# A projection's quads of v and z taken apart: v alone and z alone, with the context's v by seven products in two heads of four

## The chip, the cores and the metric

The kernel runs on one core of a Trainium2 chip. The metric is the device time of one execution in microseconds, the median of several runs. All matrix products run as float32r matmuls on TensorE; VectorE (DVE) and ScalarE (ACT) prepare their operands and drain their results; GpSimd (POOL) issues the stores of intermediate results, SyncE (SP) the loads.

## The reference

Two layers over 512 latent tokens (x) and 256 context tokens (ctx) of width 1024. Layer 0 is a bidirectional multi-scale retention with four heads, layer 1 a chunked gated MLP on the latent tokens. What matters here is the projection at the start of layer 0:

```python
def retention_project(h, w_in):
    a, bq, cq = RET_QK_WIDTH, 2 * RET_QK_WIDTH, 2 * RET_QK_WIDTH + RET_WIDTH
    q = to_heads(h @ w_in[:, :a], RET_HEADS)
    k = to_heads(h @ w_in[:, a:bq], RET_HEADS) * (RET_QK_DIM ** -0.5)
    v = to_heads(h @ w_in[:, bq:cq], RET_HEADS)
    z = h @ w_in[:, cq:]
    return q, k, v, z
```

For each head q and k have 256 columns, v and z have 512. The latent tokens need q, k, v and z. The context tokens need only k and v: layer 1 is the last one and reads no context, so the context's q, z and output are not computed.

## The kernel before

**Quads.** The projection is cut into twelve quads. A quad is a weight block of 1024 rows by 512 columns, cut in quarters B11, B12, B21, B22 of 512 x 256 (first digit: the half of the rows, second digit: the half of the columns). A quad of kind `kq` has k's columns of one head in one half and q's in the other. A quad of kind `vz` has 256 of v's columns in one half and 256 of z's in the other, so each head has two `vz` quads. `QUADS` fixes the order.

**Seven products.** The latent tokens' side is cut in quarters A11 to A22 of 256 tokens by 512 rows of the contraction. Instead of eight products of quarters a quad does seven (a Strassen-Winograd scheme): B11, B21, B22 as they are and four differences T1 to T4 of quarters, each with an operand of the tokens' side: A11, A12, A22 or one of the sums S1 to S4 (`WITH`). Class `Product` runs them in the order `SINGLE` and keeps the running sums: a `snap` is a ScalarE copy of a PSUM bank, `plus` a VectorE addition of a bank to an earlier snap; a result quarter is passed to `done`. The first quad, `kq` of head 0, is done plainly with eight products.

**The context beside it.** For `kq` and `vz` quads the context's k or v is needed for the first half of columns only. `beside` does it plainly: the context's 256 tokens (`hc`) with B11, and with B21, each a product of 24 matmuls, added in one bank.

**Halves.** Every operand of a matmul is split into a high half (ScalarE, a cast to float32r) and a low half (VectorE, what the cast left out), and every pair of 128-row operands takes three matmuls (`mm3`): low x high, high x low, high x high. So one product of quarters is 4 x 2 x 3 = 24 matmuls of 128 x 256. The weights' halves stand in one of four `hl` tiles; `Stream.upto` makes them two products ahead of their use, `Stream.sum` makes the differences T1 to T4 in place in the loaded quarters (`raw`, VectorE, 128 x 1024).

**Order of the work.** TensorE's order is that of the text. VectorE's and ScalarE's instructions of this stage are ordered by the scheduler, except for work put in with `aside`, which stays behind what stands before it in the text. After the first quad come two quads run in turns (`pair`, order `PAIRED`); there the sums S2, S3, S4 and the decay logarithms are made as well. Then a loop runs the other nine quads one by one, n = 0 to 8, and does side work between the products: `popped` (the rotary embedding, "rope", of a `kq` quad's results, mostly in the quad behind it), `step` (background: a piece of the modulation vectors, five steps in a quad), `decay(0)` at n = 5 (tables of the decays: exponentials on ScalarE, products on VectorE), `load_qk(0)` from n = 6 and `load_v(0)` at n = 8 (operands of the first head's attention).

**Stores.** `v_d`, `vc_d`, `z_d` are places in device memory, per head; `spill` stores to them through POOL's queue. z goes through SiLU on ScalarE first. Places in on-chip memory are laid out once, in the order of the calls of `lay`; a tile is named by its tag there.

Of the kernel before, what the change touches and what calls it, by code (L numbers as in the profile page):

```python
# [8 lines left out]
F32R = mybir.dt.float32r  # L9
# [4 lines left out]
P = 128  # L14
# [53 lines left out]
def hybrid_kernel(ctx, tc, xT_d, cT_d, cv_d, sv_d, rows_d, ada0_d, adag_d, w_d, rope_d, dec_d, ws_d, id_d, out_d):  # L68
# [21 lines left out]
    def lay(sizes, bufs=1):  # L90
        for tag, n in sizes.items():
# [3 lines left out]
         "sq0": 16, "sq1": 16, "sq2": 16, "rs0": 1024, "rs1": 1024, "rs2": 1024, "shb": 16, "gate0": 32, "gs1": 32,  # L95
# [59 lines left out]
    class Stream:  # L155
# [40 lines left out]
        def upto(self, n, late=None):  # L196

            while self.done < min(n, self.limit or len(self.items)):
                q, name, uses, at, place = self.items[self.done]
                self.pump()  # L200
                r = self.raws[q, at]
                self.sum(self.done)
                hl = place() if place else hl_tile(q[0] in ("vz", "v1"))
# [65 lines left out]
    QUADS = (("kq", 0), ("vz", 0, 0), ("vz", 0, 1), ("vz", 1, 0), ("vz", 1, 1), ("kq", 1), ("vz", 2, 0), ("vz", 2, 1),  # L269
             ("kq", 2), ("vz", 3, 0), ("kq", 3), ("vz", 3, 1))  # L270
# [73 lines left out]

    class Product:
# [3 lines left out]
        def __init__(self, product, done, side=None):  # L349
            self.product, self.done, self.side, self.s = product, done, side, {}  # L350

        def snap(self, key, bank):
            t = self.s[key] = t2("snap")
            act.copy(t, bank)
# [6 lines left out]
        def beside(self, name, w):  # L361
            if self.side is None:
                return
            if name == "B11":
                self.c = pt()
                self.product(self.c, self.side[:, :, 0:4, :], w, True)
            else:
                self.product(self.c, self.side[:, :, 4:8, :], w, False)
                self.done("c", self.c)

        def run(self, name, w):
            if name == "B11":
                self.x = pt()
            elif name == "B21":
                self.y = pt(tag="tm")
            elif name == "T1":
                self.z = pt(tag="tm")
            bank = getattr(self, {"B21": "y", "T1": "z", "B22": "z"}.get(name, "x"))
            self.product(bank, A[WITH[name]], w, name in ("B11", "B21", "T1"))
# [14 lines left out]
            if name in ("B11", "B21"):  # L394
                self.beside(name, w)
# [166 lines left out]
    def kq_finish(h, name, c):  # L562
        if name == "c":
            spill(kc_d[h], c if h == 0 else settled(c))
            return
# [10 lines left out]
    def vz_done(h, fh):  # L576
        fs = slice(fh * HS, fh * HS + HS)

        def done(name, c):
            if name in ("11", "21", "c"):  # L580
                dst = vc_d[h] if name == "c" else v_d[h][int(name[0]) - 1]
                s = c if name == "11" else settled(c)
                spill(dst[:, :, fs], s.rearrange("p (t n) -> p t n", t=2))
                return
            act.activation(c, c, AF.Silu)
            spill(z_d[h][int(name[0]) - 1][:, :, fs], c.rearrange("p (t n) -> p t n", t=2))
        return done

    def project(q):
# [92 lines left out]
    shb = st([P, 4], "shb")  # L682
    plain_done = kq_done(0)
    held = {}

    def hold(*keys):

        for key in keys:
            i = len(held)
            if i % 2 == 0:  # L690
                two = st([P, 2, 512], f"g{1 + i // 2}", name="held")
# [4 lines left out]
            plain_done(key if key == "c" else f"{key[0] + 1}{key[1] + 1}", two[:, i % 2, :])  # L696
# [5 lines left out]
    for kb in range(1, 8):  # L702
# [23 lines left out]
        if kb == 7:  # L726
# [3 lines left out]
            dve.tensor_tensor(shb, sh0[:, 0:4, 0], sh0[:, 4:8, 0], ALU.add)  # L730
            for k in range(4):
# [22 lines left out]


# [173 lines left out]
    two = {q: project(q) for q in pair}  # L929
    sums = {("B11", 1): sum_s2, ("T1", 0): sum_s4, ("T2", 0): sum_s3, ("B22", 0): decay_logs}  # L930
# [595 lines left out]
```

## Time and profile before

| what | value |
|---|---|
| median of 3 runs | 888.93 us (885.72 to 889.62) |
| the profiled execution's own time | 888.54 us |
| its span, first to last instruction | 886.8 us |
| granted TensorE clock | 0.999 |
| TensorE matmuls busy | 876.3 us (99%) |
| VectorE busy | 712.5 us (80%) |
| ScalarE busy | 461.5 us (52%) |
| first quad ends, the pair begins | 59.68 us |
| the pair ends, the loop over nine quads begins | 110.56 us |
| the last quad ends, attention begins | 340.98 us |

In the profile's rows PE is TensorE's matmuls, PEld its loads of the stationary operand. A row `hl<-raw,hl` on DVE is a low half, `hl<-raw` on ACT a high half, `raw<-raw` a difference of quarters, `snap<-pst,snap` an addition of a bank. A matmul row names its output, then the moving and the stationary operand's tiles: `oA`, `oS` are quarters and sums of the latent tokens, `hc` is the context. All instructions that go through the kernel's queue helper have line L54, so they are told apart by their tiles. Durations of neighbouring VectorE instructions overlap a little, so their sum can exceed the busy time of a stretch.

### The profile page before, as it was taken

To read this page: it belongs to the slowest core of one execution; us is meant where nothing else is said; L and a number is where in the kernel's file an instruction comes from. 1 tells how busy PE (TensorE), PEld (TensorE's weight loads), DVE (VectorE), ACT (ScalarE), POOL (GpSimd) and SP (SyncE) were. 2 spreads that over 40 slices of the span, in tenths; PEclk is the share of its full clock that TensorE was granted. 3 is DMA by queue.
4 is the path that set the end of the run, shared out by engine and by line. 5 is a ranking of instruction groups with operands and counts; after the bars stand their busy time and mean duration, and the time that the engine had idled before them with its cause. 6 is when DMAs were issued, how large, how long until landed. Compare 5 with 4: busy or idle time off the path is not lost.

```text
span 886.8 us, 16946 instructions
## 1 busy us (share of the span) xinstructions
PE 876.3 (99%) x6884; PEld 835.0 (94%) x6884; DVE 712.5 (80%) x996; ACT 461.5 (52%) x717; POOL 51.5 (6%) x88
## 2 busy tenths in 40 slices
PE   8999999999999999999999999999999999999997
PEld 7899999999999999998989999999999899899986
DVE  2689967699779877878676689999898488688995
ACT  5464644433554535636265549744666556256434
POOL 0001201002101101000000001011000000000000
PEclk9999999999999999999999999999999999999999
DMA  9943967457577458848345412535445135036212
GB/s 338 403 132 108 291 232 244 161 157 249 188 240 249 137 167 326 289 119 266 136 136 174 156 59 84 197 136 192 134 138 173 42 120 191 24 120 214 60 60 95
DMA packets 75486, 153.81 MB, mean 173 GB/s; under 512 B 7696, under 2 KB 34448, under 8 KB 75408
## 3 DMA queue, kind: packets, MB, share of 16 engines
q1 hardware_dynamic: 68544, 130.69, 45.0%
q0 software_dynamic: 6720, 22.03, 6.5%
q8 instruction: 54, 0.88, 0.4%
q14 instruction: 24, 0.20, 0.1%
q10 hardware_dynamic: 144, 0.01, 0.0%
HBM read 128.58 MB, written 24.12 MB: 172 GB/s over the span
## 4 chain that ended last, share of the span: by engine, by line
PE 91%; DVE 4%; ACT 3%; DMA 1%; issue 1%; SPq 0%; DVEq 0%
PE pst L54 91%; DVE hl L54 1%; DMA xq<-in_xT_dram 1%; ACT f L54 1%; ACT junk L54 1%; DVE raw L54 1%; SPq L54 0%; DVE f L54 0%; ACT hl L54 0%; ACT oA L54 0%; DVE o L54 0%; ACT xs L54 0%; DVE oS L54 0%; DVE xq L54 0%; DVE bns L54 0%
## 5 line engine op out<-in xcount | busy, mean ns | idle before, releaser
L54 DVE TENSOR_TENSOR hl<-raw,hl 128x1024 fp32r<-128x1024 f32 x193 | 234.6, 1220 | 74.8 <-ACT hl L54 74.7
L54 ACT CAST hl<-raw 128x1024 fp32r<-128x1024 f32 x193 | 201.7, 1050 | 141.7 <-PE pst L54 66.3
L54 PE MATMUL pst<-hl,oS 128*128 128x256 f32 x1152 | 135.2, 278 | 0.6 <-DVE snap L54 0.6
L54 PEld LDWEIGHTS pst<-hl,oS 128*128 128x128 f32 x1152 | 133.5, 188 | 1.9 <-ACT snap L54 0.8
L54 PE MATMUL pst<-oS,hl 128*128 128x256 f32 x1104 | 133.6, 280 | 0.7 <-ACT oS L54 0.5
L54 PEld LDWEIGHTS pst<-oS,hl 128*128 128x128 f32 x1104 | 130.2, 189 | 2.3 <-ACT oS L54 1.0
L54 PE MATMUL pst<-oA,hl 128*128 128x256 f32 x936 | 117.4, 281 | 0.2
L54 PEld LDWEIGHTS pst<-oA,hl 128*128 128x128 f32 x936 | 112.0, 189 | 2.6 <-DVE rope_b L54 0.8
L54 DVE TENSOR_TENSOR raw<-raw 128x1024 f32<-128x1024 f32 x92 | 111.7, 1217 | 0.6
L54 ACT COPY snap<-pst 128x512 f32<-128x512 f32 x92 | 53.8, 585 | 97.7 <-PE pst L54 97.3
L54 PE MATMUL pst<-og,hl 128*128 128x256 f32 x768 | 92.4, 281 | 0.0
L54 PE MATMUL pst<-hl,oA 128*128 128x256 f32 x768 | 92.2, 278 | 0.0
L54 PEld LDWEIGHTS pst<-og,hl 128*128 128x128 f32 x768 | 90.5, 189 | 0.8 <-issue 0.2
L54 PEld LDWEIGHTS pst<-hl,oA 128*128 128x128 f32 x768 | 90.0, 188 | 0.2 <-issue 0.2
L54 PE MATMUL pst<-v,ph 128*128 128x512 f32 x192 | 60.1, 394 | 0.0
L54 PE MATMUL pst<-hl,ya 128*128 128x512 f32 (+1 forms) x246 | 59.2, 386 | 0.0
L54 PEld LDWEIGHTS pst<-hl,ya 128*128 128x128 f32 x246 | 45.3, 188 | 9.5
L54 DVE TENSOR_TENSOR snap<-pst,snap 128x512 f32<-128x512 f32 x69 | 47.2, 684 | 4.6 <-PE pst L54 4.4
L54 PE MATMUL pst<-hl,hc 128*128 128x256 f32 x384 | 47.0, 278 | 0.0
L54 PEld LDWEIGHTS pst<-hl,hc 128*128 128x128 f32 x384 | 45.5, 188 | 0.0
L54 ACT CAST ph<-pf 128x512 fp32r<-128x512 f32 x24 | 14.8, 618 | 58.0 <-DVE pf L54 57.6
L54 PEld LDWEIGHTS pst<-v,ph 128*128 128x128 f32 x192 | 36.2, 188 | 7.4
(177 smaller groups left out, 1019.0 us busy)
## 6 DMA issues: line engine op xcount, KB each, us to landing
raw<-in_w_dram SPq DMA_DIRECT2D x224, 256.0 KB, 3.9
bg<-in_adag_dram SPq DMA_DIRECT2D x32, 512.0 KB, 4.2
ada_w<-in_ada_dram SPq DMA_DIRECT2D x16, 512.0 KB, 8.5
raw<-in_w_dram SPq DMA_DIRECT2D x16, 512.0 KB, 4.2
bg<-in_dec_dram SPq DMA_DIRECT2D x12, 512.0 KB, 4.2
v<-snap POOLq DMA_DIRECT2D x16, 256.0 KB, 5.0
z<-snap POOLq DMA_DIRECT2D x16, 256.0 KB, 4.9
v<-v SPq DMA_DIRECT2D x8, 512.0 KB, 4.4
```

The source lines that it names most:

```text
L54: made = op(*args, **kw)
```

## The change

The two kinds of quad are taken apart. A `vv` quad holds both halves of v's columns of one head, a `zz` quad both halves of z's; there are four of each. The context needs v for both halves of columns now, and nothing in a `zz` quad.

- The pair is `vv` of heads 0 and 1. There the context's second half of columns comes from the products that the quad has anyway: with T1 = B12 - B11 it is C1 T1 + C1 B11 + C2 B22, where C1 and C2 are the context's halves of the contraction. C1 B11 is copied to the new tile `share` (tag w7) on its way to the first half. So the context takes four products of 24 matmuls: B11, B21, T1, B22.
- In `vv` of heads 2 and 3 the context has its own seven products, with its tokens cut in 128 and 128: a second `Product` beside the first, with operands `AC` and product function `tokens_c`, 12 matmuls for each. The sums of the context's quarters are made in the pair by `sums_c`, with `shb_c` for the shift.
- The order of quads is `kq`, then `vv` 0 and 1 (the pair), then in the loop `vv` 2, `kq` 1, `vv` 3, `zz` 0, `kq` 2, `zz` 1, `zz` 2, `kq` 3, `zz` 3.
- What a quad's results go through moves with its kind: `v_done`, `vc_done`, `z_done` in place of `vz_done`.
- The context's quarters `cq` (tags g2, g3) stay until `sums_c`, so the first quad's held results move from g1, g2, g3 to g1, dec and a `t2` tile.
- One small tile, `shbc`, is laid out ahead of the large ones.

```diff
+    lay({..., "shb": 16, "shbc": 16, "gate0": 32, ...
...
-        if kind == "vz":
-            return wide_parts(16 * i + (8 if nh else 4), kh, q[2])
+        if kind in ("vv", "zz"):
+            return wide_parts(16 * i + (4 if kind == "vv" else 8), kh, nh)
...
-    QUADS = (("kq", 0), ("vz", 0, 0), ("vz", 0, 1), ("vz", 1, 0), ("vz", 1, 1), ("kq", 1), ("vz", 2, 0), ("vz", 2, 1),
-             ("kq", 2), ("vz", 3, 0), ("kq", 3), ("vz", 3, 1))
+    QUADS = (("kq", 0), ("vv", 0), ("vv", 1), ("vv", 2), ("kq", 1), ("vv", 3), ("zz", 0), ("kq", 2), ("zz", 1),
+             ("zz", 2), ("kq", 3), ("zz", 3))
...
+    def tokens_c(bank, a, w, fresh):
+        for kt in range(4):
+            mm3(bank, (a[:, 0, kt, :], a[:, 1, kt, :]), (w[:, 0, kt * HS:kt * HS + HS], w[:, 1, kt * HS:kt * HS + HS]),
+                fresh and kt == 0, kt == 3)
...
             if name == "B11":
                 self.c = pt()
-                self.product(self.c, self.side[:, :, 0:4, :], w, True)
-            else:
-                self.product(self.c, self.side[:, :, 4:8, :], w, False)
+            elif name == "T1":
+                self.c = pt()
+            a = self.side[:, :, 0:4, :] if name in ("B11", "T1") else self.side[:, :, 4:8, :]
+            self.product(self.c, a, w, name in ("B11", "T1"))
+            if name == "B11" and self.share is not None:
+                act.copy(self.share, self.c)
+            elif name == "B21":
                 self.done("c", self.c)
+            elif name == "B22":
+                dve.tensor_tensor(self.share, self.c, self.share, ALU.add)
+                self.done("c2", self.share)
...
-            if name in ("B11", "B21"):
+            if name in ("B11", "B21") or self.share is not None and name in ("T1", "B22"):
                 self.beside(name, w)
...
+    def project(q, share=None):
         if q[0] == "kq":
-            return Product(features, kq_done(q[1]), hc)
-        return Product(tokens, vz_done(q[1], q[2]), hc)
+            return [Product(features, kq_done(q[1]), hc)]
+        if q[0] == "zz":
+            return [Product(tokens, z_done(q[1]))]
+        if share is not None:
+            return [Product(tokens, v_done(q[1]), hc, share)]
+        return [Product(tokens, v_done(q[1])), Product(tokens_c, vc_done(q[1]), ops=AC)]
...
+    AC = {"A11": hc[:, :, 0:4, 0:P], "A12": hc[:, :, 4:8, 0:P], "A22": hc[:, :, 4:8, P:HS]}
+
+    def sums_c():
+        c11, c21, c12, c22 = (cq[g][:, :, i * P:i * P + P] for g in range(2) for i in range(2))
+        for n, (x, y, op_, shift) in enumerate(((c22, c21, ALU.add, shb_c), (c22, c11, ALU.subtract, sh0[:, 4:8, 1]),
+                                                (c12, c22, ALU.subtract, None), (c11, c21, ALU.subtract, None))):
+            s = AC[("S1", "S2", "S4", "S3")[n]] = st([P, 2, 4, P], f"s{n}", F32R, name="sc")
+            dve.tensor_tensor(x, x, y, op_)
+            if shift is None:
+                split((s[:, 0], s[:, 1]), x)
+                continue
+            for k in range(4):
+                shifted(x[:, k, :], shift[:, k:k + 1], s[:, 0, k, :], s[:, 1, k, :])
...
-    two = {q: project(q) for q in pair}
-    sums = {("B11", 1): sum_s2, ("T1", 0): sum_s4, ("T2", 0): sum_s3, ("B22", 0): decay_logs}
+    share = st([P, 2, 512], "w7", name="share")
+    two = {q: project(q, share[:, n, :])[0] for n, q in enumerate(pair)}
+    sums = {("B11", 1): sum_s2, ("T1", 0): sum_s4, ("T2", 0): sum_s3, ("B22", 0): decay_logs, ("T3", 0): sums_c}
...
-        pr = project(q)
+        prods = project(q)
         for i, name in enumerate(SINGLE):
-            pr.run(name, Q.get())
+            w = Q.get()
+            for pr in prods:
+                pr.run(name, w)
```

More of the change, by code (lines that the diff above doesn't have):

```diff
@@ L343, in tokens, with __init__ @@
                 mm3(bank[:, t * HS:t * HS + HS], l, r, fresh and kt == 0 and t == 0, kt == 3)
+    def tokens_c(bank, a, w, fresh):
+        for kt in range(4):
+            mm3(bank, (a[:, 0, kt, :], a[:, 1, kt, :]), (w[:, 0, kt * HS:kt * HS + HS], w[:, 1, kt * HS:kt * HS + HS]),
+                fresh and kt == 0, kt == 3)
     class Product:
-        def __init__(self, product, done, side=None):
-            self.product, self.done, self.side, self.s = product, done, side, {}
+        def __init__(self, product, done, side=None, share=None, ops=None):
+            self.product, self.done, self.side, self.share, self.s = product, done, side, share, {}
+            self.ops, self.n, self.tag = (A, 512, "tm") if ops is None else (ops, HS, "ps")
         def snap(self, key, bank):
-            t = self.s[key] = t2("snap")
+            t = self.s[key] = t2("snap", (P, self.n))
             act.copy(t, bank)
@@ L574, in kq_finish, with v_done, vc_done, done @@
         spill(dst[h][th], a)
-    def vz_done(h, fh):
-        fs = slice(fh * HS, fh * HS + HS)
+    def v_done(h):
         def done(name, c):
[L580 to L586, printed above, removed]
-        return done
-    def project(q):
-        if q[0] == "kq":
-            return Product(features, kq_done(q[1]), hc)
-        return Product(tokens, vz_done(q[1], q[2]), hc)
+            if name[0] == "c":
+                dst, nh, c = vc_d[h], len(name) - 1, settled(c) if name == "c" else c
+            else:
+                dst, nh, c = v_d[h][int(name[0]) - 1], int(name[1]) - 1, settled(c) if name == "21" else c
+            spill(dst[:, :, nh * HS:nh * HS + HS], c.rearrange("p (t n) -> p t n", t=2))
+        return done
+    def vc_done(h):
+        def done(name, c):
+            if name == "21":
+                t = t2("snap", (P, HS))
+                act.copy(t, c)
+                c = t
+            nh = int(name[1]) - 1
+            spill(vc_d[h][:, int(name[0]) - 1, nh * HS:nh * HS + HS], c)
+        return done
+    def z_done(h):
+        def done(name, c):
+            t = t2("snap") if name == "21" else c
+            act.activation(t, c, AF.Silu)
+            nh = int(name[1]) - 1
+            spill(z_d[h][int(name[0]) - 1][:, :, nh * HS:nh * HS + HS], t.rearrange("p (t n) -> p t n", t=2))
+        return done
+    def project(q, share=None):
+        if q[0] == "kq":
+            return [Product(features, kq_done(q[1]), hc)]
[4 more added lines that the diff above has]
+        return [Product(tokens, v_done(q[1])), Product(tokens_c, vc_done(q[1]), ops=AC)]
     f11, f12, f21, f22 = xq[0, 0], xq[0, 1], xq[1, 0], xq[1, 1]
@@ L682, in hybrid_kernel @@
     shb = st([P, 4], "shb")
+    shb_c = st([P, 4], "shbc")
     plain_done = kq_done(0)
@@ L689, in hold @@
             i = len(held)
+            if key == "c":
+                t = t2("held")
+                act.copy(t, bank[key])
+                spill(kc_d[0], t)
+                continue
             if i % 2 == 0:
-                two = st([P, 2, 512], f"g{1 + i // 2}", name="held")
+                two = st([P, 2, 512], ("g1", "dec")[i // 2], name="held")
             else:
@@ L695, in hold @@
             act.copy(two[:, i % 2, :], bank[key])
[L696 removed]
+            plain_done(f"{key[0] + 1}{key[1] + 1}", two[:, i % 2, :])
     sq[2] = st([P, 2, 2], "sq2", name="sq")
```

16 lines of the change are left out of this document (9 added, 7 removed).

## The prediction

> **What bounds the kernel now.** I read the page first (engine shares), then the chain of waits, then busy time of each engine by stretches cut at the quad boundaries, then the timeline of TensorE. The page says that TensorE is busy for nearly all of the span:
>
> ```profile
> span 886.8 us, 16946 instructions
> PE 876.3 (99%) x6884; PEld 835.0 (94%) x6884; DVE 712.5 (80%) x996; ACT 461.5 (52%) x717; POOL 51.5 (6%) x88
> ```
>
> The chain that ended last, in order of time, holds one piece which covers everything the change touches after the first quad:
>
> ```profile
> 57.65 471.54 PE pst L54 x3741
> ```
>
> From 57.65 us on, through the other eleven quads and the attention, the end is set by TensorE alone, without a gap for 471.54 us. A matmul taken out there shortens the run by its pitch, as long as VectorE and ScalarE can still deliver the halves of the weights in time. That is read from the stretches. The first row is the pair of quads, then one row for each quad of the single loop, n = 0 to 8 (before: v with z, v with z, kq 1, v with z twice, kq 2, v with z, kq 3, v with z):
>
> ```profile
> core 0: us, PE busy (x) PEld busy (x) DVE busy (x) ACT busy (x) POOL busy (x), PEclk, DMA share, GB/s
> 59.68:110.56 50.88, 50.88 (x434) 50.88 (x433) 49.88 (x72) 32.14 (x45) 8.73 (x14) 1.00 0.56 178
> 110.56:136.00 25.44, 25.44 (x218) 25.44 (x217) 17.67 (x18) 11.02 (x14) 3.02 (x5) 1.00 0.62 216
> 136.00:161.44 25.44, 25.44 (x218) 25.44 (x217) 20.87 (x20) 10.94 (x14) 3.38 (x5) 1.00 0.69 238
> 161.44:188.56 27.12, 27.12 (x227) 25.95 (x225) 18.99 (x23) 10.25 (x13) 2.45 (x4) 1.00 0.42 137
> 188.56:213.06 24.50, 24.50 (x219) 24.50 (x217) 22.61 (x29) 10.46 (x13) 3.24 (x6) 1.00 0.78 248
> 213.06:239.34 26.28, 26.28 (x226) 25.12 (x225) 21.50 (x23) 12.38 (x17) 4.52 (x7) 1.00 0.64 202
> 239.34:264.78 25.44, 25.44 (x219) 25.44 (x217) 20.76 (x25) 13.89 (x19) 1.77 (x3) 1.00 0.77 237
> 264.78:290.35 25.57, 25.57 (x222) 24.60 (x220) 25.28 (x31) 13.98 (x18) 3.81 (x6) 1.00 0.70 227
> 290.35:316.48 26.13, 26.13 (x222) 25.93 (x221) 22.33 (x29) 10.94 (x15) 2.32 (x4) 1.00 0.37 122
> 316.48:340.98 24.50, 24.50 (x218) 24.50 (x217) 16.04 (x22) 9.90 (x13) 3.81 (x7) 1.00 0.74 258
> ```
>
> TensorE never waits, but VectorE is full in two rows: the pair (49.88 of 50.88 us) and n = 6 (25.28 of 25.57 us). The change moves TensorE time between quads, so these two rows decide. The granted clock is 1.00 throughout and plays no part.
>
> **The matmuls.** In the timeline TensorE's 128x256 matmuls run at two pitches, each kept for a whole quad:
>
> ```profile
> 82.29 22.78 PE L54 MATMUL pst<-hl,oS 128*128 128x256 f32 x192
> 104.91 8.64 PE L54 MATMUL pst<-hl,oA 128*128 128x256 f32 x72
> 180.07 5.82 PE L54 MATMUL pst<-oS,hl 128*128 128x256 f32 x48
> 185.73 2.99 PE L54 MATMUL pst<-oA,hl 128*128 128x256 f32 x24
> 194.02 5.60 PE L54 MATMUL pst<-hl,oS 128*128 128x256 f32 x48
> 199.46 2.88 PE L54 MATMUL pst<-hl,oA 128*128 128x256 f32 x24
> ```
>
> From one start to the next: (104.91 - 82.29)/192 = 117.8 ns in the pair, (185.73 - 180.07)/48 = 117.9 ns in a kq quad, (199.46 - 194.02)/48 = 113.3 ns in a quad of the single loop that comes after a kq quad. By the row lengths of n = 0 and 1 (25.44 us for 216 matmuls) the slower pitch went on from the pair until the first kq quad.
>
> A quad's seven products for x are 7 x 24 = 168 matmuls; the context adds 2 x 24 = 48, so each v-with-z quad has 216. After it: v of heads 0 and 1 four context products, 168 + 96 = 264; v of heads 2 and 3 seven products of 12, 168 + 84 = 252; z 168. The eight quads go from 8 x 216 = 1728 to 528 + 504 + 672 = 1704. That is 24 fewer, or 2.7 to 2.8 us. If the pitches stay with their places, 117.8 holds for the pair, the v quad behind it and the three kq quads (528 + 252 + 648 = 1428, before 1512), and 113.3 for the rest (924, before 864): 1428 x 0.1178 + 924 x 0.1133 = 272.9 us against 1512 x 0.1178 + 864 x 0.1133 = 276.0 us. **Saved: 3.1 us.** The Trainium skill (TensorE: Matmul & The Clock Gate, Back-to-back issue gap) gives N / 2.4 + 2.5 ns for an isolated gap, 109 ns at N = 256, and so 2.6 us for the 24; the trace's pitches are both above that, and I use the trace.
>
> **The pair.** It grows from 432 to 528 matmuls, to 528 x 0.1178 = 62.2 us, 11.3 us longer. VectorE gets the sums of the context's quarters (sums_c) and two additions into share. The nearest rows, and those for the later quads, are the groups of n = 6 by form (count, busy us, mean ns) and two groups of the whole run:
>
> ```profile
> L54 DVE TENSOR_TENSOR hl<-raw,hl 128x1024 fp32r<-128x1024 f32 x7 | 8.4, 1219 | 0.0
> L54 DVE SCALAR_TENSOR_TENSOR ada_a<-bg,cpad,ada_a 128x1024 f32<-128x1024 f32 x5 | 6.4, 1278 | 0.0
> L54 DVE TENSOR_TENSOR raw<-raw 128x1024 f32<-128x1024 f32 x4 | 4.9, 1216 | 0.0
> L54 DVE TENSOR_TENSOR snap<-pst,snap 128x512 f32<-128x512 f32 x3 | 2.1, 686 | 0.3 <-PE pst L54 0.3
> L54 DVE TENSOR_TENSOR rope_a<-rope_a,rope_b 128x256 f32<-128x256 f32 x4 | 1.5, 418 | 0.0
> L54 DVE TENSOR_TENSOR qk<-qk 128x512 fp32r<-128x512 f32 x2 | 1.4, 684 | 0.0
> L54 DVE SCALAR_TENSOR_TENSOR hc<-cq,sh,hc 128x256 fp32r<-128x256 f32 x8 | 3.4, 480 | 0.2 <-ACT hc L54 0.2
> L54 ACT CAST hl<-raw 128x1024 fp32r<-128x1024 f32 x193 | 201.7, 1050 | 141.7 <-PE pst L54 66.3 <-DVE raw L54 53.8 <-issue 12.3
> ```
>
> sums_c is four sums of 512 elements and two subtractions of 512 (6 x 0.684), and eight shifted subtractions of 128 (at most 8 x 0.48); share is 2 x 0.684: at most 9.3 us. That is below the 11.3 us that the pair gains, so I take it as hidden; the cover ends if less than 2 us of it is left, and then the first product of n = 0 that needs a sum (T1) waits. Its ScalarE work hides too (32.14 of 50.88 us busy).
>
> **The z quads.** Here the cover shrinks. A z quad has 168 x 0.1133 = 19.0 us of TensorE, and a VectorE list that hardly changes: seven low halves, four differences, three additions. The order after is n = 0 v, 1 kq, 2 v, 3 z, 4 kq, 5 z, 6 z, 7 kq, 8 z, while the side work is tied to n or to the quad behind a kq: three ropes in the quad after each kq, five background steps in each quad, decay(0) at n = 5, the halves of q and k from n = 6. So n = 5 now has the ropes and decay(0) in a z quad.
>
> Durations in a full queue overlap: the rows of n = 6 that are shown, with six more rope multiplications of 512 (6 x 0.684), come to 8.4 + 6.4 + 4.9 + 2.1 + 1.5 + 1.4 + 4.1 = 28.8 us, and the stretch was busy 25.28 us, a factor of 0.88. A quad's own 15.4 us (8.4 + 4.9 + 2.1) are then 13.5 us; three ropes (each 2 x 0.684 + 2 x 0.418 = 2.2) 5.8; a half of q or k 0.6; a background step at most 1.28 x 0.88 = 1.1, of which eight in twelve touch VectorE, so 3.8 for five. decay(0) and its table loads:
>
> ```profile
> L54 DVE TENSOR_TENSOR dt<-bg 128x512 f32<-128x512 f32 x8 | 5.5, 691 | 6.2 <-ACT bg L54 6.2
> L54 DVE TENSOR_TENSOR dt<-bg 128x384 f32<-128x384 f32 x4 | 2.2, 559 | 1.9 <-ACT bg L54 1.9
> L54 ACT ACT_TABLE_LOAD x16 | 20.5, 1283 | 1.5 <-PEq L1515 1.2
> 242.97 1.28 ACT L54 ACT_TABLE_LOAD   x1
> 244.26 1.34 ACT L54 ACTIVATE bg<-bg,lg 128x512 f32<-128x512 f32 x2
> ```
>
> The dt rows are four heads: (5.5 + 2.2)/4 x 0.88 = 1.7 us for one.
>
> n = 3: 13.5 + 3.8 = 17.3 of 19.0 us, fits. n = 5: 13.5 + 3.8 + 5.8 + 1.7 = 24.8 of 19.0, short by 5.8. n = 6: 13.5 + 3.8 + four halves 2.4 = 19.7 of 19.0, short by 0.7. n = 7 (kq, 25.4 us) recovers. n = 8: the list of the old n = 8 less the context's share, at most 16.04 of 19.0, fits, and the hand-over to attention keeps its last three products. So VectorE falls behind by 6.5 us over n = 5 and 6. Against that stands the lead: the low halves run ahead of their use. n = 4 is a kq quad with some 5 us of VectorE to spare, so the lead is full when n = 5 begins: four hl tiles let a split begin when three products (3 x 2.72 us) lie ahead of it, less one cast and one subtraction (1.05 + 1.22), about 5.9 us. The tightest lead of the full stretch before was at the T1 product of n = 7:
>
> ```profile
> 292.11 2.35 DVE L54 TENSOR_TENSOR hl<-raw,hl 128x1024 fp32r<-128x1024 f32 x2
> 296.59 5.92 PE L54 MATMUL pst<-oS,hl 128*128 128x256 f32 x48
> ```
>
> Its low half is the first of the two and ended about 293.3, so 3.3 us were left. 6.5 less 5.9 leaves 0.6 us of stall, less 3.3 leaves 3.2 us; none if ropes and background steps slip behind the splits. From both sides: 0 to 6.5 us, and ScalarE can add to it. Exp of decay(0) now falls among the Silu of a z quad, which makes exp, silu, exp, silu where exp and silu lay in different quads: two more loads, 2 x 1.28 = 2.6 us, in a quad whose ScalarE work would be about 13.89 us plus four Silu. That fits 19.0 us but can delay a cast. So 0 to 9.1 us; I take **1.5 us**, near the lower row, because the lead is full on entry. The Trainium skill (ScalarE: Activation LUTs, What ACT_TABLE_LOAD costs) counts a drain of 1380 ns besides the load's 1283, so 5.3 us for the two, and an upper end 2.7 us higher; here the activation began 1.29 us after the load did (242.97 to 244.26), so the trace has no such drain.
>
> The rest has one answer: the loads are the same bytes, vc is spilled in eight half-size pieces for two heads, on POOL, which is busy for under a fifth of each stretch; the held tiles change places only.
>
> **Sum.** 888.5 (the profiled execution's own time; its span is 886.8, and the median of the runs, 888.93, is 0.4 above) - 3.1 + 1.5 = **886.9 us**, within 0.5% of before. That bound, 4.4 us, is about what a measurement of this kernel can tell from no change. This case's own range, with the stall from 0 to 6 and the saving at 2.7 to 3.1: 885 to 892.
>
> **The rivals.** *The stall decides (slower).* VectorE's queue is in order; the ropes and steps tied to n = 5 stand in front of later splits, dt waits for the exps (6.2 and 1.9 us idle in the rows above, for four heads), and the lead is gone by n = 6. The price is the upper end, 9.1 us, plus (6.2 + 1.9)/4 = 2.0 us of such waits: 888.5 - 3.1 + 11.1 = 896.5 us. It decides from a stall of 7.5 us. For it: VectorE was full at n = 6 with 25.6 us of cover, and now has 19.0. Against: no gap arose there, and n = 4 stands in front with time to spare.
>
> *The faster pitch spreads (faster).* If the pair and the v quad behind it run at 113.3, 780 x 0.0045 = 3.5 us more are saved: 888.5 - 3.1 - 3.5 = 881.9 us without a stall, 883.4 with one. For it: the pitch changes where operands change roles, and the new 12-matmul products put new switches there. Against: the change into the pair is the same as before.
>
> *The places in memory (either sign).* A small tile (shbc) comes ahead of all large ones, and all of them move by the same amount. That places matter is shown by the only products whose weights' halves stand in other tiles:
>
> ```profile
> 549.90 6.00 PE L54 MATMUL pst<-hl_e,oA 128*128 128x256 f32 x48
> ```
>
> 48 take 6.00 us here and 5.60 us in the row at 194.02, so 0.4/48 = 8 ns more each, about 121 ns. As the distances stay the same I expect nothing; if all matmuls of the quads went to one of the two pitches, that is 924 x 0.0045 = 4.2 us slower or 1428 x 0.0045 = 6.4 us faster.
>
> *It does not do what it says.* The count of 24 follows from the loops; only a slower pitch for the runs of 12 could eat it: 168 x 0.008 = 1.3 us at 121 ns.
>
> **The chances.** The likeliest case 0.46 (nearly all within 0.5%, 0.02 slower), the stall 0.23, the faster pitch 0.23, the places 0.08, half each way. Faster 0.27, same 0.44, slower 0.29. The range leaves out the end of the stall case and the best of the pitch case: 881 to 896 us.
>
> **What would show it.** Right: stretches of about 62 us for the pair and 29 us for each v quad, 19 to 20 us for each z quad, no gap before T1 of n = 0, and at n = 5 and 6 VectorE at nine tenths or more with under 3 us of TensorE idle behind VectorE's hl. Four table loads among exp and silu at n = 5. Wrong: a piece of DVE hl or ACT bg of several us in the chain between 200 and 300 us; the pair at 113 ns; or any change after 341 us.

## The result, and the profile after

The changed kernel takes **894.92 us** (median of 6 runs, 894.16 to 896.29) against 888.95 us for the kernel before in the same runs: a ratio of 1.007, 95% interval 1.005 to 1.0089. It is slower by 0.7%. The forecast was 886.9 us, no change beyond half a per cent; the range, 881 to 896 us, holds the time at its upper end. The rival *The stall decides* named 896.5 us.

The profiled execution took 895.1 us, its span is 893.3 us, 6.5 us more than before. The page of the kernel after gives span and busy times:

```profile
span 893.3 us, 16960 instructions
PE 878.2 (98%) x6860; PEld 835.8 (94%) x6860; DVE 722.1 (81%) x1019; ACT 465.3 (52%) x729; POOL 53.1 (6%) x92
```

24 matmuls fewer (6884 to 6860), and yet TensorE is busy 1.9 us longer. The chain that ended last (start, length, what), where before there was one piece of 471.54 us, now breaks at 262.92 us. These are its longer pieces up to the point where TensorE alone goes on:

```profile
57.96 204.96 PE pst L54 x1749
...
265.31 5.17 DMA bg<-in_dec_dram
...
270.50 0.69 DVE snap L54
271.19 1.13 DVE hl L54
...
272.83 1.22 DVE raw L54
...
275.86 1.13 DVE raw L54
...
278.85 2.27 DVE hl L54 x2
...
283.46 1.15 DVE hl L54
```

The stretches cut at the quads of the kernel after say which quads these are. The rows are the pair, vv 2 (n = 0), zz 0 (n = 3), zz 1 and zz 2 (n = 5 and 6), zz 3 (n = 8):

```profile
core 0: us, PE busy (x) PEld busy (x) DVE busy (x) ACT busy (x) POOL busy (x), PEclk, DMA share, GB/s
59.99:122.19 62.20, 62.20 (x531) 62.20 (x530) 59.36 (x91) 33.19 (x52) 10.36 (x16) 1.00 0.49 160
122.19:151.21 29.02, 29.02 (x254) 29.02 (x253) 20.17 (x21) 11.95 (x16) 4.64 (x8) 1.00 0.53 165
...
207.22:226.26 19.04, 19.04 (x170) 19.04 (x169) 16.56 (x17) 11.22 (x14) 2.97 (x5) 1.00 0.84 274
...
253.27:274.05 20.78, 19.22 (x170) 19.05 (x169) 18.67 (x27) 14.99 (x19) 2.46 (x4) 1.00 0.71 225
274.05:298.75 24.70, 21.82 (x171) 20.99 (x169) 24.70 (x28) 15.37 (x21) 3.27 (x5) 0.93 0.83 274
...
325.75:344.81 19.06, 19.06 (x171) 19.06 (x170) 15.82 (x22) 9.20 (x12) 2.99 (x5) 1.00 0.80 287
```

A zz quad without a stall takes 19.05 us. Zz 1 and zz 2 take 20.78 + 24.70 = 45.48 us, so **7.4 us of stall** lie in n = 5 and 6. The whole projection stage, from the start of the pair to the start of attention, grew from 281.30 to 284.82 us. Without the stall it would be 277.4 us. In these two quads no instruction of VectorE or ScalarE waits for a load of weights, so the DMA of the weights is not what is late. Of the rest of the difference, attention became 1.3 us longer (201.81 to 203.14), and the stage behind it 1.4 us (79.82 to 81.20); the last needs no cause in the change, as the kernel before shows the longer time too in another execution (below).

How the stall arises is read from three engines' timelines of the kernel after. First TensorE (start, length, instruction; in brackets the idle time before it and who ended it):

```profile
264.17 5.60 PE L54 MATMUL pst<-hl,oS 128*128 128x256 f32 x48
271.33 5.71 PE L54 MATMUL pst<-hl,oA 128*128 128x256 f32 x48 [1.56 <-DVE snap L54]
277.44 0.38 PE L54 MATMUL pst<-hl,oS 128*128 128x256 f32 x1 [0.40 <-ACT hl L54]
280.04 4.46 PE L54 MATMUL pst<-hl,oS 128*128 128x256 f32 x24 [2.22 <-DVE hl L54]
284.65 2.90 PE L54 MATMUL pst<-hl,oS 128*128 128x256 f32 x23 [0.15 <-DVE hl L54]
```

VectorE, some rows of the same time:

```profile
254.60 1.23 DVE L54 TENSOR_TENSOR hl<-raw,hl 128x1024 fp32r<-128x1024 f32 x1 [0.29 <-ACT hl L54]
...
259.48 0.69 DVE L54 TENSOR_TENSOR dt<-bg 128x512 f32<-128x512 f32 x1 [1.79 <-ACT bg L54]
...
262.75 1.22 DVE L54 TENSOR_TENSOR hl<-raw,hl 128x1024 fp32r<-128x1024 f32 x1
...
266.90 0.69 DVE L54 TENSOR_TENSOR rope_b<-snap,rope 128x512 f32<-128x512 f32 x1
267.50 1.22 DVE L54 TENSOR_TENSOR hl<-raw,hl 128x1024 fp32r<-128x1024 f32 x1
268.63 0.76 DVE L54 TENSOR_TENSOR rope_a<-rope_a,rope_b 128x256 f32<-128x256 f32 x2
269.30 1.28 DVE L54 SCALAR_TENSOR_TENSOR ada_a<-bg,cpad,ada_a 128x1024 f32<-128x1024 f32 x1
270.50 0.69 DVE L54 TENSOR_TENSOR snap<-pst,snap 128x512 f32<-128x512 f32 x1
...
278.76 2.36 DVE L54 TENSOR_TENSOR hl<-raw,hl 128x1024 fp32r<-128x1024 f32 x2
...
292.12 1.22 DVE L54 TENSOR_TENSOR hl<-raw,hl 128x1024 fp32r<-128x1024 f32 x1
```

ScalarE:

```profile
271.22 0.64 ACT L54 ACTIVATE snap<-snap 128x512 f32<-128x512 f32 x1 [3.81 <-DVE snap L54]
271.87 1.28 ACT L54 ACT_TABLE_LOAD   x1
...
274.53 1.28 ACT L54 ACT_TABLE_LOAD   x1
...
276.36 1.03 ACT L54 CAST hl<-raw 128x1024 fp32r<-128x1024 f32 x1
```

Until 255.83 us all is as the prediction had it: that low half (the row at 254.60) is by the order of the products B21's, whose first matmul is at 261.45, so the lead was 5.6 us. Then VectorE makes no low half for 6.9 us: its queue holds a difference, a rope, a dt product that waits 1.79 us for an exp, and a background step. The next low half, T3's, ends at 263.97, and T3 begins at 264.17: 0.2 us of lead are left. The first stall, at T4, is not even at a low half: T4 accumulates into the bank of T3, which T3's `plus` (the row at 270.50) must read first. That `plus` can start only when T3's 24 matmuls are done, at 264.17 + 24 x 0.1133 = 266.9 us, and only one product, B22 (2.7 us), lies between T3 and T4. It can never be further ahead than that, whatever lead the low halves have; here most of a rope, a low half and a background step stood before it (the rows from 266.90), and it started 3.6 us after T3's end. Behind it ScalarE had waited 3.81 us for the same `plus`; then come a table load, exps, a table load, and the cast for T1 of zz 2 at 276.36. Its low half, the first of the two in the row at 278.76, ends at 279.99 us, and TensorE starts 2.22 us late.

### The profile page after: what moved, and what is told of

It reads as the page before. It is cut to its first block, busy times and chain, and to the rows that moved or that the text cites. A ratio compares the mean times of both kernels' runs of the same rounds, so it can differ in the third digit from the quotient of the medians.

```text
span 893.3 us, 16960 instructions
## 1 busy us (share of the span) xinstructions
PE 878.2 (98%) x6860; PEld 835.8 (94%) x6860; DVE 722.1 (81%) x1019; ACT 465.3 (52%) x729; POOL 53.1 (6%) x92
## 4 chain that ended last, share of the span: by engine, by line
PE 86%; DVE 6%; ACT 4%; DMA 2%; issue 1%; SPq 0%; DVEq 0%; ACTq 0%
PE pst L54 86%; DVE hl L54 2%; DMA xq<-in_xT_dram 2%; DVE raw L54 1%; ACT hl L54 1%; ACT f L54 1%; ACT junk L54 1%; DMA bg<-in_dec_dram 1%; DVE snap L54 1%; DVE f L54 0%; DVE rope_a L54 0%; ACT oA L54 0%; DVE o L54 0%; DVE ada_a L54 0%; DVE rope_b L54 0%
## 5 line engine op out<-in xcount | busy, mean ns | idle before, releaser
L54 PE MATMUL pst<-hl,oS 128*128 128x256 f32 x1152 | 139.5, 281 | 3.0 <-DVE hl L54 2.4
L54 PEld LDWEIGHTS pst<-hl,oS 128*128 128x128 f32 x1152 | 136.6, 190 | 4.7 <-DVE hl L54 2.8
L54 ACT COPY snap<-pst 128x512 f32<-128x512 f32 x90 | 50.8, 565 | 76.9 <-PE pst L54 76.8
L54 DVE TENSOR_TENSOR snap<-pst,snap 128x512 f32<-128x512 f32 (+1 forms) x75 | 49.6, 665 | 3.8 <-PE pst L54 3.4
L54 DVE SCALAR_TENSOR_TENSOR ada_a<-bg,cpad,ada_a 128x1024 f32<-128x1024 f32 x28 | 35.9, 1280 | 6.2 <-DMA bg<-in_adag_dram 6.2
L54 DVE SCALAR_TENSOR_TENSOR acc<-pst,gate,acc 128x256 f32<-128x256 f32 x64 | 29.1, 479 | 11.8 <-PE pst L54 11.7
```

Of the source, the lines that this page charges most:

```text
L54: made = op(*args, **kw)
```

## Experiments

The theories: **V**, VectorE's list at n = 5 and 6 is longer than two z quads. **T**, exp among Silu: table loads and exps stand in front of casts in ScalarE's queue. **D**, the decay's third load comes too late. **L**, the small tile `shbc` moved all large tiles. Times are ratios to the kernel before, and the length of the projection stage in the one profiled execution (before 281.30, after 284.82 us). A gap is counted here from start to start, less the pitch of the matmuls between; that is up to 0.16 us more than the idle time in a row's brackets, because a matmul's length in the rows overlaps the next start.

**Places, both ways.** The kernel before with the small tile, and the kernel after with that tile laid out last:

```diff
-    lay({..., "shb": 16, "gate0": 32, ...
+    lay({..., "shb": 16, "shbc": 16, "gate0": 32, ...
```

> The kernel before with nothing but the small tile shbc laid out ahead of the large ones. If the moved places cost the 2.7 us that the part behind the projection lost: 891.5 us, with the v1 stage (542 to 622 us) at 118 ns per matmul instead of 113. If they cost nothing: 889.0 us, and the slower pitch there has to come from what ran before it.

> The changed kernel with shbc laid out last, so that all other tiles stand where they stood before. Places theory: 892.2 us, the v1 stage back at 113 ns. Otherwise 894.9 us. The gaps at n = 5 and 6 stay at about 7.4 us in both.

Measured: 0.9997 (0.9988 to 1.0007), projection 281.30 us; and 1.005 (1.0037 to 1.0064), 284.95 us with the same gaps. L falls for the projection: the places cost nothing there. They do cost something in the attention: it takes 202.42 us in the first of these profiles (201.81 in the kernel before) and 202.29 us in the second (203.14 in the kernel after). These 0.6 to 0.9 us are too little for the ratios to show.

**The kernel before once more.**

> The kernel before, once more. If the stages behind the projection (attention 201.8 us, the first gated product 79.8 us at a median pitch of 113 ns in the first profile) vary from execution to execution, this profile shows either 113 or 117 ns there, and an attention between 201.8 and 202.5 us, as the kernel before with the small tile moved did (202.4 and 80.8 us at 117 ns). If the pitch is fixed by the program, it shows 113 ns and 201.8 us again. The projection stage is 281.3 us by both.

The stage behind the attention, first in the profile before, then in this one:

```profile
542.79:622.61 79.82, 79.19 (x687) 78.52 (x685) 77.57 (x105) 47.87 (x72) 10.28 (x19) 1.00 0.47 162
```

```profile
542.67:624.03 81.36, 81.09 (x687) 80.78 (x685) 78.12 (x106) 47.83 (x72) 10.28 (x19) 1.00 0.48 159
```

The same program takes 79.8 or 81.4 us there, at a median pitch of 113 or 118 ns. So the same 1.4 us come and go without the change; what decides about the pitch is not shown.

**The decay one quad earlier, and no background steps in the two z quads.**

```diff
-            if n == 5 and i % 2 == 0:
+            if n == 4 and i % 2 == 0:
```

```diff
-            if 2 not in pieces and i not in (2, 4):
+            if 2 not in pieces and i not in (2, 4) and n not in (5, 6):
```

> The changed kernel with decay(0) in the kq quad n = 4 instead of the z quad n = 5. If the gaps come from VectorE's total work at n = 5 and 6: 1.7 us of tables and the 1.8 us idle before them go, so 3.5 of 7.4 us come back, 891.4 us. If they come from the alternation of exp and silu in one quad (table loads and exps ahead of casts in ScalarE's queue): nearly all comes back, 888 us.

> The changed kernel without background steps at n = 5 and 6 (they follow later). If VectorE's work there decides: 10 steps, of which two in three are an instruction of 1.28 us with an overlap of an eighth, are 7.5 us less, so the gaps go and 887.5 us are left. If the exps and table loads decide: 2 us at most come back, 893 us.

Measured: 1.0015 (1.0006 to 1.0023), projection 281.48 us; and 1.0069 (1.0056 to 1.0082), 286.57 us. Moving the decay wins 3.3 of the 7.4 us. Without the steps the first gap (at T4) goes, but a gap of 1.9 us at 277 us stays, and the steps, now at n = 7 and 8, make new gaps of 1.0 and 2.3 us there. That run alone could not decide: it showed that something other than the steps holds the second gap (in its chain two table loads and exps stand in front of the cast), and that late steps are no cure.

**Exp replaced by Silu, tables gone.** The right tables of head 0's decay are left out.

```diff
-            act.activation(e[:, 0:512], e[:, 0:512], AF.Exp, scale=lg[:, h:h + 1])
+            act.activation(e[:, 0:512], e[:, 0:512], AF.Silu if h == 0 else AF.Exp, scale=lg[:, h:h + 1])
...
```

> The change, with Silu in the place of Exp for the decay tables of head 0 (so right values of these tables are left out): the same instructions in the same order, without the two extra table loads and with the exps replaced by activations of the same size. Theory T (the table switches delay the casts in ScalarE's queue): the stall of 7.4 us in the two z quads falls by the loads of 1.28 us each, to 3 to 5 us, time about 1.002 to 1.004 of before. Theory V: at most 1 us is won, stall 6 to 7.4 us, time 1.004 to 1.007 of before.

Measured: 1.0063 (1.0045 to 1.0082), projection 284.88 us, gaps of 1.04, 0.37, 1.78 and 1.84 us. T as the only cause falls: without the extra loads the time is the same.

**No ropes in zz 1.** Head 2's q and k are stored unrotated.

```diff
+        if h == 2:
+            spill(dst[h][th], settled(c) if name == "21" else c)
+            return
```

> The change, with the ropes of head 2 left out (its q and k stored unrotated): VectorE's list of n = 5 shrinks by 5.8 us, decay, exps, table loads and background steps stay. If VectorE's list is what is too long: shortage of 43.4 - 38.1 = 5.3 us is gone, the stall of 7.4 us (with the slow clock behind it) falls to 0 to 2 us, projection 277.5 to 280 us, time 0.998 to 1.002 of before. If ScalarE's queue (exp, table loads, casts behind them) or the DMAs that the decay waits for decide, the stall stays at 4 us or more, projection 281.5 us or more.

Measured: 1.0047 (1.0032 to 1.0062), projection 283.30 us. V alone falls as well: some 5.8 us of VectorE's work (the prediction's sum for three ropes) are gone and only 1.5 us are won. In ScalarE's timeline of this kernel stands what holds now:

```profile
271.12 1.28 ACT L54 ACT_TABLE_LOAD   x1 [2.71 <-DMA bg<-in_dec_dram]
```

The decay has two buffers for three table loads. The third is asked for at its second step only; in the chain of waits it is issued at 264.20 us, behind the second exps and a cast, and lands 6.85 us later. The exps that need it stand in ScalarE's queue, and the casts behind them wait too. (Whether the buffer or the place in SyncE's queue behind two weight loads delays the issue is not told apart: the next kernel changes both.) In the kernel after this load was under way from 265.31 and the `plus` at 270.50 came as late: two chains that end together.

**A third buffer, alone and together with no ropes, and with Silu besides** (leaving out what the two kernels above leave out):

```diff
-    dec0 = decay(0, ("g0", "s3"))
+    dec0 = decay(0, ("g0", "s3", "w7"))
...
-            for j in range(len(es), min(i + 2, 3)):
+            for j in range(len(es), 3 if h == 0 else min(i + 2, 3)):
```

> The change, with a third buffer for the decay's tables of head 0 (w7), so that all three loads are issued at its first step; in the change the third load waits until the second exps have read theirs, is issued at 265.3 us and lands at 271 us, and its exps stand in ScalarE's queue ahead of the casts. Theory V + D (two chains, VectorE's list and this load, meet at 270.5 to 271 us): VectorE's list stays, so the plus at 270.50 us stays late and only what came behind it gets better: 0.5 to 2.5 us won, projection 282.3 to 284.3 us. Theory D alone (the load decides): nearly all is won, projection 278 to 280 us. Theory V alone: nothing, 284.8 us.

> The change without the ropes of head 2 (its q and k stored unrotated) and with the third buffer: both chains away. Without the ropes alone the projection was 283.30 us, with gaps of 2.0 and 1.1 us behind exps that had waited for the load, and 2 us at the slow clock behind them. Theory V + D: those gaps go, projection 278 to 279.5 us. If the two extra table loads (2.6 us in ScalarE's queue) hold the casts by themselves, 1 to 2 us of stall remain, 279.5 to 281 us; if something else decides, 282 us or more.

> As the kernel without head 2's ropes and with the third buffer (projection 280.78 us, 2.35 us of gaps left), and Silu in the place of Exp for the decay tables of head 0 as well (their right values are left out): no table switches at n = 5. If the switches hold the casts of the second z quad (in that kernel exps and two loads fill ScalarE from 268.81 to 272.75 us and the cast follows at 273.29), the 2.35 us fall to 0 to 0.8 us, projection 278.4 to 279.3 us. If VectorE's background steps in front of the low halves do it, 1.5 us or more stay, 280 us or more.

Measured: 1.005 (1.0033 to 1.0068), 1.0011 (0.9998 to 1.0024), 1.0007 (0.999 to 1.0024). The first kernel's profiled execution ran the pair at the faster pitch, as its row shows. The row stops three matmuls short of the pair's end: the whole pair took 59.9 us, and with the quad behind it 88.6 us, 2.6 us less than the same work in the kernel after (91.2 us).

```profile
60.05:119.60 59.55, 59.55 (x528) 59.55 (x527) 58.41 (x91) 33.05 (x52) 10.57 (x16) 1.00 0.48 158
```

With that added back, the projection is:

| | third load late | third buffer | and no table switches |
|---|---|---|---|
| ropes in zz 1 | 284.82 us | 282.65 + 2.6 = 285.2 us | not tried |
| no ropes | 283.30 us | 280.78 us | 279.92 us |

With ropes the third buffer wins nothing; without them it wins 2.5 us, and the ropes are worth 1.5 us with the late load and 4.4 us without it. So V and D hold side by side, and in these executions each hides the other. The left column holds a time at the slow clock (last section), the others hold none; that does not make the difference, because the product behind it had to wait for its low half all the same (until 284.65 and 282.67 us). The medians of all runs say the same less sharply: in the order of the table 1.007 and 1.005 with ropes, 1.0047 and 1.0011 without. Each alone wins 0.2%, both together 0.6%, but the intervals are too wide to show that the whole is more than its parts. The switches come third, 0.9 us between two executions (a gap of 0.5 us goes). What is then left is one gap, in TensorE's timeline of the last kernel:

```profile
279.42 2.88 PE L54 MATMUL pst<-hl,oS 128*128 128x256 f32 x23 [1.72 <-DVE hl L54]
```

The low half that it waits for ends at 279.37 us; in front of it VectorE made two differences, a background step and another low half without a break, from 273.55 us on. So the last gap is VectorE's list again.

**What the 24 matmuls are worth.** In vv of heads 2 and 3 the context by four products of 24 again, without `sums_c`; in the loop's order of products this adds up other sums for the context's second half of columns, so only its time counts.

> The change, with the context of v in heads 2 and 3 also by four products of 24 instead of seven of 12, and without sums_c: what the 24 matmuls are worth in the place where they were saved. As predicted they cost 24 x 0.113 to 0.118 = 2.7 to 2.8 us: the two vv quads of the loop about 1.4 us longer each, the stall at n = 5 and 6 as before. If the matmuls by the context's own quarters (slower, 118 to 120 ns) eat part of the gain, 2.0 to 2.4 us. If the saved products only move the stall (VectorE sets the end from n = 2 on), 0 to 1 us in total. Time 1.007 to 1.009 of before by the first, 1.005 by the last.

Measured: 1.009 (1.0071 to 1.0109), projection 289.74 us, 4.9 us longer. 0.9 us of this is more time at the slow clock and 0.6 us longer gaps at n = 6; the rest, 3.4 us, is near the 2.7 to 2.8 us of the matmuls (2.1 us of it in vv 2 and 1.2 us in vv 3, where they were put back). The saving was real and was not swallowed.

**Side work where VectorE has time.** Three attempts: decay at n = 4 with more steps at n = 0 and 2 and fewer at n = 5 and 6; the change's own order with decay at n = 1 and seven steps at n = 1 and 4, two at n = 5 and 6; and other orders of quads.

```diff
-            if 2 not in pieces and i not in (2, 4):
+            if 2 not in pieces and (n in (0, 2) or i in (0, 3) or n not in (5, 6) and i not in (2, 4)):
```

> The change, with decay(0) in the kq quad n = 4 and with three of the ten background steps of n = 5 and 6 moved to n = 0 and 2, which have cover. Theory V (VectorE's queue holds more than a z quad's 19 us at n = 5 and 6): with the decay away 0.5 to 1.5 us of stall was left, with fewer steps it goes too: the projection at 278 to 280 us, time 0.990 to 0.999 of before (881 to 889 us), since 24 matmuls fewer are then worth their 2.7 to 3.1 us. Theory T (only exp among silu costs): as with the decay moved alone, projection 281.5 us, time 1.0015 of before. If the steps are late by their own loads, new gaps show behind a DMA row at n = 0 or 2.

> The change, in its own order of quads, with side work moved into the kq quads, which have VectorE time to spare: decay(0) at n = 1, seven background steps at n = 1 and 4, two at n = 5 and 6 (the decay's second buffer is w7, free there). VectorE's list at n = 5: 13.5 + 5.8 + 1.5 = 20.8 of 19.0 us, at n = 6: 13.5 + 1.5 + 2.4 = 17.4 of 19.0. If VectorE's list decides and its lead is whole on entry: no stall, projection 278.2 us, time 0.995 to 0.998 of before. If the lead counts for nothing (the plus and the casts have none): 1 to 2 us of stall, time 0.998 to 1.000.

Measured: 1.0037 (1.0024 to 1.005), 281.92 us; and 1.0004 (0.9993 to 1.0016), 280.37 us with gaps of 1.2 us at n = 4 and 1.5 us at n = 6. The first was a wrong choice: with the decay and the ropes behind it, VectorE had no idle time from 245 to 284 us, and gaps of 2.2 and 2.0 us arose in the z quads.

The orders, first alone, then with the decay at n = 2 (buffers `g0` and `w7`) and seven steps at n = 0 and 2, four at n = 1, 3, 4 and 5, and at last with two at n = 1 and 3 and five at n = 4 and 5:

```diff
-    QUADS = (("kq", 0), ("vv", 0), ("vv", 1), ("vv", 2), ("kq", 1), ("vv", 3), ("zz", 0), ("kq", 2), ("zz", 1),
-             ("zz", 2), ("kq", 3), ("zz", 3))
+    QUADS = (("kq", 0), ("vv", 0), ("vv", 1), ("kq", 1), ("vv", 2), ("kq", 2), ("vv", 3), ("zz", 0), ("zz", 1),
+             ("kq", 3), ("zz", 2), ("zz", 3))
```

> The change with another order of the quads in the loop: kq 1, vv 2, kq 2, vv 3, zz 0, zz 1, kq 3, zz 2, zz 3. Ropes of two kq quads then stand in vv quads (29 us of TensorE) and none in a quad with the decay. Theory V: n = 5 needs 13.5 + 3.8 + 1.7 = 19.0 of 19.0 us, n = 7 (zz 2 with ropes and halves of q and k) 13.5 + 3.8 + 5.8 + 1.2 = 24.3 of 19.0, short by 5.3 us, which is about the lead of 5.9: stall 0 to 2.5 us, projection 278 to 281 us, time 0.992 to 1.001 of before. Theory T: exp, silu, exp, silu stands in zz 1 all the same (two extra loads), so most of the stall of 7.4 us stays: time 1.004 to 1.007 of before.

> The other order of quads (kq 1, vv 2, kq 2, vv 3, zz 0, zz 1, kq 3, zz 2, zz 3) with side work in the kq quads: decay(0) at n = 2, seven steps at n = 0 and 2, four in the vv and the first zz quads. VectorE has no quad with a longer list than TensorE's but zz 2 (ropes: 13.5 + 5.8 + 1.2, steps done, 20.5 of 19.0 us). If VectorE's list decides: projection 278 us, at most 1 us of stall, time 0.995 to 0.998 of before, both kernels beaten. If stalls remain, their place shows what else binds: with DMA rows in the chain, the background loads.

> The other order with side work in the kq quads (projection 279.21 us, gaps of 0.78 us at n = 3, where VectorE was busy for 28.80 of 28.80 us, and 0.34 us at n = 4), now with two steps in the vv quads and five in the z quads behind them. If VectorE's list is what stalls there, n = 3 has 2 x 1.1 us less of it and the gap goes: projection 278.1 to 278.6 us, time 0.997 to 0.998 of before. If the steps are only late then and stall at n = 5 to 7, 279 us or more.

Measured: 1.0023 (1.0011 to 1.0035), with gaps of 0.9 us at n = 4 and 2.5 us at n = 6 (projection 280.10 us, with the pair at the faster pitch, 59.9 us); **0.9983 (0.9974 to 0.9991)**, median 887.35 us; 0.9991 (0.9978 to 1.0004). The second beats both kernels, by little. A stretch of its vv 3 (n = 3), where VectorE has no pause, and its whole projection:

```profile
203.50:232.30 28.80, 28.18 (x243) 27.98 (x242) 28.80 (x37) 10.03 (x13) 5.26 (x9) 1.00 0.82 282
...
60.04:339.25 279.21, 278.33 (x2379) 274.57 (x2377) 245.13 (x308) 135.86 (x187) 38.92 (x63) 1.00 0.64 212
```

Two gaps, 0.78 and 0.34 us, are left; without them it would be 278.1 us, 3.2 below before. That is the saving of 3.1 us that the prediction had worked out. The last kernel took the gap at n = 3 away, as V expects, and got one of 1.5 us at n = 7 in its place; its projection of 277.05 us holds a pair at the faster pitch (59.9 us in place of 62.2), so it is no gain.

## Why the prediction was wrong

**The matmuls** (right). 24 fewer, the pair 62.20 us (forecast 62.2), vv 2 29.0, zz 0 and zz 3 19.04 and 19.06 us (19.0); the best version shows 3.2 us of saving (3.1), and putting the 24 back cost about 3.4 us. In the kernel after itself the projection less the stall is 3.9 us shorter; 0.7 us of the surplus lie in vv 2, where the sum had 252 x 0.1178 = 29.7 us.

**The pair's cover** (right). VectorE was busy for 59.36 of 62.20 us, and no gap arose in it or before T1 of n = 0.

**VectorE's list at n = 5 and 6** (right). Forecast 24.8 + 19.7 = 44.5 us of work, measured 18.67 + 24.70 = 43.4 us, against 38.1 us of TensorE. Only the sum is right; by quad, more of the work fell into the second.

**The stall of 1.5 us** (the step that failed; it measured 7.4 us). The working was "6.5 less 5.9 leaves 0.6 us of stall", with the lead of the low halves as a buffer that the shortage must use up first. The lead was there, 5.6 us, but it did not protect. First, VectorE's list was 5.3 us longer than TensorE's (43.4 - 38.1), and VectorE stood idle for another 2.1 us (1.79 of it in the wait for the exp), which the working had only in a rival's price. (That the two make 7.4 us is bookkeeping: busy and idle time of a stretch always add up to the stretch.) Secondly, a `plus` cannot be ahead by more than one product; the prediction looked at the low halves only, and T4's bank waited for a `plus` that stood behind a rope and a step. Thirdly, the lead was not used up in the end: while TensorE stood, VectorE made it anew. The low half at 292.12, by the order of the program's instructions that of kq 3's first product, ends 6.5 us ahead of 299.80, where that product begins (that of zz 2's last product, made after it, ends only 0.7 us ahead). So the lead paid for next to nothing of the shortage. Fourthly, the wait of the decay for its own third load was priced at a quarter of 8.1 us as one rival's extra; it is a second chain that by itself, without ropes, holds 2.5 us.

**The rival that won.** *The stall decides* has its mechanism (ropes and steps in front of the splits, dt waiting for exps), but its price is too high: 9.1 + 2.0 = 11.1 us against 7.4. That its 896.5 us come so near the measured 894.9 is partly luck, because 2.7 us arose behind the projection, which it did not count. "The lead is gone by n = 6" was true already at T3 of n = 5. "n = 4 stands in front with time to spare" was the argument against it, and it was worthless once the queue's order within the quad put 6.9 us of other work in a row. *The faster pitch spreads* did not hold for the change as such: the pair's pitch varies by execution. *The places* were refuted both ways for the projection; for the attention see below.

**After 341 us** (wrong, by little). Attention is 1.3 us longer in the profile, and the profiles of the other kernels part this in two. Where nothing disturbs its start, it takes 202.41 to 202.42 us with the small tile ahead of the large ones (the kernel before with that tile, and the three kernels with the other order of quads) and 201.64 to 201.81 us without it (the kernel before, twice). So some 0.7 us go with the places, where the prediction expected nothing; why, is not shown. In the change's own order two short waits at the hand-over are new: the first product with v begins 4.81 us behind the start of the stage, before 4.24, which makes 0.6 us. The kernel after with the tile laid out last has these waits alone, and 202.29 us.

## What to carry to other kernels

A lead of prepared operands covers only the operation that has it: list every instruction of the full queue that can't be done early (here the `plus` between two products into one bank), and price there what stands in front of it. When work of one kind leaves a stage and another stage gets shorter, the side jobs tied to the index of the loop must be laid out again by the time that each new stage leaves on its second engine; together with another order of the quads that turned 0.7% slower into 0.2% faster here. Where taking one suspect away wins little, take two away together before clearing either.

## What the runs showed of the hardware

**The clock after a stall.** Stretches of 2 us of the kernel after, in and behind the gap at 277.8 us:

```profile
278.00:280.00 2.00, 0.00 (x0) 0.00 (x0) 2.00 (x3) 2.00 (x3) 0.93 0.76 268
```

```profile
280.00:282.00 2.00, 1.96 (x9) 1.96 (x10) 2.00 (x2) 0.25 (x1) 0.00 (x0) 0.50 0.98 223
282.00:284.00 2.00, 2.00 (x15) 2.00 (x15) 2.00 (x3) 1.04 (x1) 0.00 (x0) 0.71 0.52 211
```

The granted clock (the third column from the end) fell to a half for 0.28 + 2.00 + 1.16 = 3.4 us, and 24 matmuls took 4.46 us there. With the third buffer the same place had the same gap, and the clock stayed up, 23 matmuls in 2.88 us:

```profile
277.49 2.88 PE L54 MATMUL pst<-hl,oS 128*128 128x256 f32 x23 [2.21 <-DVE hl L54]
280.83 0.38 PE L54 MATMUL pst<-hl,oS 128*128 128x256 f32 x1 [0.47 <-ACT hl L54]
282.10 2.89 PE L54 MATMUL pst<-hl,oS 128*128 128x256 f32 x23 [0.88 <-DVE hl L54]
```

The slow matmuls are part of the 7.4 us, some 1.6 us of it. They did not add to them: with the clock up, TensorE came to the next product earlier and waited there for its high and its low half. From the second matmul of T1 to the second of T2 it is 4.61 us in both kernels (280.04 to 284.65 us here, 277.49 to 282.10 there). The Trainium skill (TensorE: Matmul & The Clock Gate, What's actually happening) has the clock halved after at least one idle window of about 3.4 us, in windows that run freely. The length of the slow time fits, and so does that the same gap counts in one kernel's execution and not in another's; but 2.6 us without more than one matmul were enough here, less than that window.

**The pitch of one program.** The pair took 62.2 us in the kernel after and 59.9 us with the third buffer, from the same code up to there, and the stage behind the attention 79.82 or 81.36 us in the kernel before. Which of the two pitches, 113 or 118 ns, a stage has can change from execution to execution; a single profile can mislead by 1.5 to 2.6 us, nearly as much as this change saves.
